# Seven products in place of eight for four rows of a mixer, and weight sums made by transfers

## The chip, the cores and the metric

The kernel runs on one core of a Trainium2 chip. The metric is the device time of one launch in microseconds (us). The core has five engines that run side by side and wait for one another by semaphores: PE (TensorE, matmuls), DVE (VectorE), ACT (ScalarE), POOL (GpSimd, here mostly an issuer of transfers) and SP (SyncE, here only an issuer of transfers).

## The reference, cut to what matters

Two layers of a streaming encoder. Each layer is a half-step feed-forward net, a mixer, and a second half-step feed-forward net. The mixer computes, with `h = RMSNorm(x)` and `z = h @ w_in` split into columns for the convolution, the attention and the gates:

```python
g = jax.nn.sigmoid(g + b_gate)
g_conv, g_attn = jnp.split(g, 2, axis=-1)
y_conv, conv_new = _short_conv(cb, cc, cv, conv_prev, w_conv)
...
y_attn, k_new, v_new = attn_fn(q, k, v)
y_attn = y_attn.reshape(b, t, ATTN_W)
m = g_conv * (y_conv @ w_conv_out) + g_attn * (y_attn @ w_attn_out)
return m @ w_o, conv_new, k_new, v_new
```

There are 640 tokens (512 of a new stream and 8 x 16 of running ones), 1024 model columns, and 512 columns each of convolution and attention. All is float32.

## The kernel before

**Tiling.** Activations lie transposed: 128 columns of the model on the partitions, the 640 tokens (`T`) along the row, in two halves of 320 (`HT`). The eight row tiles of the model are numbered m = 0 to 7. Each float32 operand is split into a high part that the matmul reads exactly (`hi`, made by a cast on ACT) and the remainder (`lo`, made by a subtraction on DVE), and a product is the sum of three matmuls: hi x hi, hi x lo, lo x hi.

**Weights.** All weights come through one stream `wst` of slabs, each 128 x 1024 float32 (512 KB, eight 128 x 128 tiles), which SP loads into three `raw` buffers in the order in which they are used. `load` issues the transfer; `source` says which pieces make up the i-th slab that PE uses; `prep` issues the casts to `whi`; `flush` the subtractions to `wlo`; `slab` hands out the next one and prepares two further ones; `ahead` asks for the sources of the one after that.

**Products by seven.** Where two row tiles of output are computed together, the kernel replaces the eight half-width products of a 2 x 2 block scheme by seven (Winograd's form of Strassen's method). Such a unit has two raw slabs ("mix" in the list of slabs) and four slabs for PE: the first raw slab as it is, two sums of weights, one sum and one plain half, and the last plain half. It also needs sums and differences of the activations (`N6`, `T5`, `T7`, `T4`), made once in a layer. In `source`, a unit of a mixer makes four 512-wide sums on DVE. Many units of the feed-forward nets (`lean`) have one of their sums made by two transfers on POOL, the second of which adds into the tile that the first has filled (`lend`).

**The stage in question.** `outputs` runs after attention, once in each layer. Its scheduled engines are PE, DVE and ACT: they work in the order in which the code issues, and POOL and SP follow by their waits. It has two kinds of step:

- `gate_pair(m)`: two row tiles of gates by seven products, `block` being one of them (12 matmuls); copies c1, u2 and c5 on ACT, additions and a multiplication by `rr` (the inverse norm) on DVE, then two sigmoids on ACT.
- `out(m)`: a plain product of a row tile, `product(py, y)`, with 4 x 3 x 2 = 24 matmuls; then DVE multiplies it by its gate. For m below 8 it is the convolution and goes into `mm[m]`; for m from 8 it is the attention and is added to `mm[m - 8]`. `py` has two PSUM buffers (`acc`).

The order is: gate pair 2; plain products 0 to 3; then for m = 4, 6, ..., 14 a gate pair m and the plain products m and m + 1. `take` splits the operands of the plain products into hi and lo, inside gate pair 2 for the convolution and inside gate pair 8 for the attention; `give` does it with `mm` for the product with `w_o` that follows (`po`). `mm[0]` to `mm[3]` reuse the convolution's own tiles `ycs`, and `mm[4]` to `mm[7]` are two spare tiles.

Of the kernel before, what the change touches and what calls it, by code (L numbers as in the profile page):

```python
# [16 lines left out]
P = 128  # L17
# [40 lines left out]
ROWS = (1, 2)  # L58

MARGIN = 2, 4  # L60
LEAN = {"a0": (1, 6), "b0": (1, 5), "a1": (0, 5), "b1": (1, 5)}

XT4, XN6, XT7, X21, X22, X11, XT5 = range(7)
# [50 lines left out]
def mixer_order():  # L114

    mix = lambda *rows: ("mix", rows)
    out = [("v", None)] + [mix(("q", p), ("k", p)) for p in range(AW // P)]
    for c in range(0, CT, 2):  # L120
        out += [mix(("C", c + i), ("V", c + i)) for i in range(2)] + [mix(("B", c), ("B", c + 1))]
    gates = [mix(("g", m), ("g", m + 1)) for m in range(0, 2 * KT, 2)]
    out += gates[:2] + [("co", m) for m in range(4)]
    for i, g in enumerate(gates[2:]):
        name, m = ("co", 4 + 2 * i) if i < 2 else ("ao", 2 * i - 4)
        out += [g, (name, m), (name, m + 1)]
    return out + [("o", m) for m in range(KT)]


# [6 lines left out]
def stages():  # L136

    out, done = [], []

    def end(kind):  # L140
        done.append((kind, out[:]))
        out.clear()

    def plain(n):
        out.extend([8] * (n // 8) + [n % 8] * (n % 8 > 0))

    def ffn(name):
        held = 0
        for what, a in ffn_order(name):
            if what == "gu":  # L150
                plain(held)
                held = 0
                out.append("gu")
            elif what == "std":
                held += 2 * KT
            elif what == "cut":
                plain(held)
                held = 0
            elif what == "rows":
                plain(held)  # L160
                held = 0
                out.append("gu")
            elif what == "ends":
                held += KT * len(a)
            else:
                held += sum(len(js) for _, js in a)
        plain(held)

    for l in range(L):
        ffn(f"a{l}")  # L170
        end("ffn")
        held = 0
        for what, _ in mixer_order():
            if what == "mix":
# [21 lines left out]
def trunk(ctx: ExitStack, tc: tile.TileContext, xin, wst, small, pbias, samplebias, kcache, vcache, gfin,  # L196
# [54 lines left out]
    for kind, units in stages():  # L251
        n = sum(2 if z in ("gu", "mix") else 1 for z in units)
        if kind == "ffn":
            inner.update(range(at + MARGIN[0], at + n - MARGIN[1]))
        at += n
    raws, ready = [], []
    sums, pool, spool = {}, [None], [None]
    lent, lean, at = {}, set(), 0
    for name, (_, units) in zip([f"{k}{l}" for l in range(L) for k in "amb"], stages()):
        ns = []  # L260
        for z in units:
            if z == "gu":
                ns.append(at)
            at += 2 if z in ("gu", "mix") else 1
        if name in LEAN:
            lean.update(ns[slice(*LEAN[name])])

    def lend(n):

        z = lent[n] = pool[0].tile([P, 2, HT], F32, tag="cap", name=f"lent{n}", bufs=6).rearrange(  # L270
            "p a b -> p (a b)")[:, h1]
        POOL.dma_start(z, wst[n][:, h1])
        POOL.dma_start(z, wst[n + 1][:, h1], accum_op=ALU.add)

    def load(i):
        while len(raws) <= i:
# [16 lines left out]
    def source(i):  # L293

        if i >= len(slabs):
            return None
        if i not in sources:
            kind, n, arg = slabs[i]
            ra = load(n)
            if kind == "plain":  # L300
                sources[i] = [(ra, slice(0, arg))]
            elif arg == 0:
                if n in lean and n not in lent:
                    lend(n)
                sources[i] = [(ra, whole)]
            else:
                rb = load(n + 1)
                if arg == 1 and kind == "gu":
                    if n + 2 in lean:
                        lend(n + 2)  # L310
                    st = sums[n] = pool[0].tile([P, CH], F32, tag="s65", name=f"s65_{n}", bufs=1)
                    add(st[:, h2], rb[:, h1], rb[:, h2])
                    add(st[:, h1], st[:, h2], ra[:, h1])
                    sources[i] = [(st, whole)]
                elif arg == 1:

                    flush()
                    st = sums[n] = spool[0].tile([P, CH // 2], F32, tag="s6", name=f"s6_{n}", bufs=1)
                    add(ra[:, h1], ra[:, h1], rb[:, h1])
                    add(st, ra[:, h1], rb[:, h2])  # L320
                    add(rb[:, h1], rb[:, h1], rb[:, h2])
                    sources[i] = [(st, h1), (rb, h1)]
                elif arg == 2:
                    if kind == "gu" and n not in lean:
                        add(ra[:, h1], ra[:, h1], rb[:, h1])
                    add(ra[:, h2], sums.pop(n)[:, h1], ra[:, h2])
                    sources[i] = [(lent.pop(n), h1), (ra, h2)] if n in lean else [(ra, whole)]
                else:
                    sources[i] = [(rb, h2)]
        return sources[i]  # L330

    pending = []
# [984 lines left out]
    def mixer(l, after):  # L1317
        with tc.tile_pool(name=f"yp{l}", bufs=1, reuse_waits="tile") as yp, \
# [84 lines left out]
            with tc.tile_pool(name=f"gp{l}", bufs=1, reuse_waits="tile") as gp, \  # L1403
                 tc.manual_schedule(engines=ORDERED):
                hold[0] = True
                mo = outputs(l, gp, ops.X, st, cs, ycs, yas, sigmoid, gates)
        ex = after()
        with tc.manual_schedule(engines=ORDERED):
            hold[0] = True
# [56 lines left out]
        def t5(self, kp):  # L1466
            self.parts(*(z[:, HT:] for z in self.h[2 * kp]), self.a[kp][:, 1])

    def outputs(l, gp, X, st, cs, ycs, yas, sigmoid, gates):
# [4 lines left out]
        mm = ycs + [spare[i // 2][:, i % 2] for i in range(CT)]  # L1474
# [4 lines left out]
        def gate_pair(m, then=None):  # L1479
# [5 lines left out]
            ACT.copy(c1, pa)  # L1485
# [7 lines left out]
            ACT.copy(u2, pa)  # L1493
            block(pc, s1, 1, XT5, every, True, True)
            ACT.copy(c5, pc)
            s2 = slab(True)[0]
# [5 lines left out]
            if then:  # L1502
                then()
            block(pc, s2, 1, X22, every, False, True)
            add(u[:, t2], pc, u2)
            s3 = slab(True)[0]
            DVE.tensor_tensor(out=u, in0=u, in1=rr, op=ALU.mult)
# [5 lines left out]
            DVE.tensor_tensor(out=g[:, t1], in0=pa, in1=rr[:, t1], op=ALU.mult)  # L1513
            sigmoid(g, m + 1, -1.0)
            flush()

        def parts(pool, tag, name, src):
# [3 lines left out]

        def out(m, y, then=None):

            py = acc(f"py{l}_{m}")
            product(py, y)
            if then:
# [7 lines left out]
            flush()  # L1534

        yc, ya, mo = [], [], []

        def take(y, name, srcs):
            for c, src in enumerate(srcs):
                y.append(parts(gp, f"y{c}", f"{name}{l}_{c}", src))  # L1540

        def give(ms):
            for m in ms:
                mo.append(parts(hp, "h", f"m{l}_{m}", mm[m]))

        gate_pair(2, lambda: take(yc, "yc", ycs))
        for m in range(4):
            out(m, yc)
        for m in range(4, 2 * KT, 2):
            last = m == 2 * KT - 2  # L1550
            gate_pair(m, (lambda: take(ya, "ya", [yas[:, c, :] for c in range(CT)])) if m == KT else
                      (lambda: give(range(1))) if last else None)
            y = yc if m < KT else ya
            out(m, y, (lambda: give(range(1, 4))) if last else None)
            out(m + 1, y, (lambda: give(range(4, 6))) if last else None)
        give(range(6, KT))
        return mo

# [518 lines left out]
def _stream(i):  # L2077
# [9 lines left out]
    for l in range(L):  # L2087
# [36 lines left out]
        for what, m in mixer_order():  # L2124
            if what == "v":
                out.append(v.reshape(KT // 2, 2, P, AW).transpose(0, 2, 1, 3).reshape(-1, P, CH))
            elif what == "mix":
                out.append(chunks(held))
                held = []

                out.append(chunks([rows[name][a][o::2] for name, a in m for o in range(2)]))
            else:
                held.append(rows[what][m])
        out.append(chunks(held))
# [71 lines left out]
```

## Time and profile before

| | us |
|---|---|
| three runs | 2488.77, 2489.51, 2489.75 |
| median | 2489.51 |
| the profiled execution | 2488.93 |
| its span, first to last instruction | 2487.1 |
| DVE busy in the span | 2140.1 |
| ACT busy in the span | 1355.4 |

The profile is of one execution. Times inside it count from the first instruction. A row of a timeline has start, length, engine, line, operation and tiles, and in square brackets how long the engine stood idle before it and what ended that. A busy PE isn't PE at its peak, since the ends of matmuls are modelled and they overlap; starts are better than durations there. The mean granted clock of TensorE was 0.999.

### The profile page before, as it was taken

The numbers are of one execution on the slowest core, as the hardware profiler recorded it, in microseconds if no ns is written. First come the engines' busy times: TensorE is split into PE (matmuls) and PEld (weight loads), VectorE is DVE, ScalarE is ACT, GpSimd is POOL, SyncE is SP. The second block draws the span as 40 slices with busy tenths as digits, with TensorE's granted clock in tenths as the row PEclk, the third lists the DMA queues.
The fourth block names the chain that finished last, engine by engine and source line by source line (L and its number), as shares of the span: only waits on it lengthen the run. The fifth ranks groups of instructions, "written<-read, shape, count | busy, mean of one in ns | idle before, by whom it ended". The sixth has DMA issues, their size and how long they took to land.

```text
span 2487.1 us, 43918 instructions
## 1 busy us (share of the span) xinstructions
PE 2473.8 (99%) x17312; PEld 2421.2 (97%) x17312; DVE 2140.1 (86%) x3533; ACT 1355.4 (54%) x2152; POOL 298.4 (12%) x451
## 2 busy tenths in 40 slices
PE   9999999999999999999999999999999999999999
PEld 8999999889999999999999999998999999999998
DVE  7999998888776899998799999988886769999997
ACT  6555556665444655555665555556644455555555
POOL 0111112211000001111001011121110000111111
PEclk9999999999999999999999999999999999999999
DMA  4443545335223333444334443453442232444444
GB/s 155 126 118 101 124 118 121 113 108 174 77 82 114 93 102 105 113 117 117 111 93 109 110 118 101 116 128 106 133 157 86 77 111 87 109 116 105 113 117 117
DMA packets 109934, 279.75 MB, mean 112 GB/s; under 512 B 12480, under 2 KB 52032, under 8 KB 109728
## 3 DMA queue, kind: packets, MB, share of 16 engines
q1 hardware_dynamic: 69552, 220.10, 28.0%
q0 software_dynamic: 39744, 56.60, 12.3%
q8 instruction: 135, 2.21, 0.4%
q14 instruction: 71, 0.58, 0.1%
q10 hardware_dynamic: 432, 0.25, 0.0%
HBM read 231.09 MB, written 7.94 MB: 96 GB/s over the span
## 4 chain that ended last, share of the span: by engine, by line
PE 94%; DVE 3%; ACT 2%; issue 1%; DMA 1%; SPq 0%; DVEq 0%; ACTq 0%; POOLq 0%
PE pab L442 12%; PE paa L442 11%; PE pcb L442 6%; PE daa L1127 6%; PE pca L442 5%; PE dab L1127 5%; PE po L418 5%; PE py L418 5%; PE qa L442 4%; PE pbb L442 3%; PE dca L1127 3%; PE pba L442 3%; PE dcb L1127 2%; PE ma_cv L442 2%; PE ma_qk L442 2%; PE pv L1612 2%
## 5 line engine op out<-in xcount | busy, mean ns | idle before, releaser
L352 DVE TENSOR_TENSOR wlo<-raw,whi 128x1024 fp32r<-128x1024 f32 (+1 forms) x569 | 579.9, 1021 | 155.9 <-ACT whi L347 152.8
L347 ACT CAST whi<-raw 128x1024 fp32r<-128x1024 f32 (+1 forms) x569 | 504.7, 890 | 380.1 <-PE pbb L442 47.2
L347 ACT CAST whi<-s 128x1024 fp32r<-128x1024 f32 (+1 forms) x158 | 150.3, 951 | 296.1 <-issue 111.2
L442 PE MATMUL pab<-xhib,whi 128*128 128x320 f32 x704 | 217.7, 309 | 0.0
L442 PE MATMUL pab<-xhib,wlo 128*128 128x320 f32 x704 | 217.3, 309 | 0.0
L442 PE MATMUL pab<-xlob,whi 128*128 128x320 f32 x704 | 217.3, 309 | 0.0
L442 PE MATMUL paa<-xhia,whi 128*128 128x320 f32 x640 | 197.8, 309 | 0.2 <-DVE ga L287 0.2
L442 PE MATMUL paa<-xhia,wlo 128*128 128x320 f32 x640 | 197.6, 309 | 0.0
L442 PE MATMUL paa<-xloa,whi 128*128 128x320 f32 x640 | 197.5, 309 | 0.0
L352 DVE TENSOR_TENSOR wlo<-s,whi 128x1024 fp32r<-128x1024 f32 (+1 forms) x158 | 173.5, 1098 | 4.6 <-ACT whi L347 4.6
L1149 POOL DMA_DIRECT2D x<-c_a x80 | 70.2, 1030 | 574.1 <-ACT ahia L1031 205.4
L442 PEld LDWEIGHTS pab<-xhib,whi 128*128 128x128 f32 x704 | 132.2, 188 | 0.9 <-issue 0.9
L1149 POOL DMA_DIRECT2D x<-c_b x72 | 63.2, 1013 | 582.0 <-ACT ahib L1031 205.6
L442 PEld LDWEIGHTS pab<-xlob,whi 128*128 128x128 f32 x704 | 132.2, 188 | 0.0
L442 PEld LDWEIGHTS pab<-xhib,wlo 128*128 128x128 f32 x704 | 132.2, 188 | 0.0
L442 PEld LDWEIGHTS paa<-xhia,whi 128*128 128x128 f32 x640 | 120.1, 188 | 1.1 <-DVE ga L287 0.5
L442 PEld LDWEIGHTS paa<-xloa,whi 128*128 128x128 f32 x640 | 120.2, 188 | 0.3 <-DVE xloa L686 0.3
L442 PEld LDWEIGHTS paa<-xhia,wlo 128*128 128x128 f32 x640 | 120.1, 188 | 0.2
L442 PE MATMUL pcb<-xhib,wlo 128*128 128x320 f32 x352 | 108.9, 309 | 0.0
L442 PE MATMUL pcb<-xlob,whi 128*128 128x320 f32 x352 | 108.6, 309 | 0.0
L442 PE MATMUL pcb<-xhib,whi 128*128 128x320 f32 x352 | 108.6, 309 | 0.0
L287 DVE TENSOR_TENSOR raw<-s,raw 128x512 f32<-128x512 f32 x158 | 107.9, 683 | 0.0
(764 smaller groups left out, 8077.7 us busy)
## 6 DMA issues: line engine op xcount, KB each, us to landing
raw<-in_wst SPq DMA_DIRECT2D x375, 512.0 KB, 3.6
x<-c_a POOLq DMA_DIRECT2D x80, 160.0 KB, 4.7
x<-c_b POOLq DMA_DIRECT2D x72, 160.0 KB, 3.6
lent<-in_wst POOLq DMA_DIRECT2D x36, 256.0 KB, 3.9
kc<-in_kcache SPq DMA_DIRECT2D x32, 256.0 KB, 4.9
vc<-in_vcache SPq DMA_DIRECT2D x16, 512.0 KB, 4.9
x<-u_a POOLq DMA_DIRECT2D x40, 160.0 KB, 3.9
x<-u_b POOLq DMA_DIRECT2D x36, 160.0 KB, 3.9
```

Source lines behind the costliest of these rows:

```text
L287: DVE.tensor_tensor(out=out, in0=a, in1=b, op=op)
L347: ACT.copy(hi[:, d], src[:, c])
L352: DVE.tensor_tensor(out=lo, in0=src, in1=hi.bitcast(F32), op=ALU.subtract)
L418: PE.matmul(ps[:, a, :HT], w, x[a] if isinstance(x, tuple) else x[:, a * HT : (a + 1) * HT], start=first and j == 0 and not seeded, stop=l ...
L442: PE.matmul(ps, a, b, start=start and kp == 0 and j == 0, stop=stop and kp == NP - 1 and j == 2, skip_group_check=True)
L1127: PE.matmul(ps[u], w, y, start=start and i == 0 and j == 0, stop=i == 1 and j == 2, skip_group_check=True)
L1149: POOL.dma_start(x[ms[2 * u + r]][:, cols], z[:, u], accum_op=ALU.add)
L1612: PE.matmul(pv[t], xx[:, t * P : (t + 1) * P], w[:, kk * AW : (kk + 1) * AW], start=c == 0 and kk == 0 and j == 0, stop=c == KT // 2 - 1 a ...
```

## The change

**Order.** `mixer_order` puts the convolution's rows 4 to 7 together after gate pairs 4 and 6, as one unit `("rows", ("co", (4, 5, 6, 7)))` that is laid out and listed as a seven-product unit. The order of the stage becomes: gate pair 2; plain products 0 to 3; gate pair 4; gate pair 6; the rows unit; then four times a gate pair (8, 10, 12, 14) and two plain products. The weight bytes of the stream stay the same.

**The rows unit.** `rows` computes four output rows by seven products of 12 matmuls over half the tokens, in place of four plain products. The stages s1, s2 and s5 hold what ACT copies out of PSUM; DVE adds and multiplies by the gates in place, and ACT copies the four results to `mm[4]` to `mm[7]` at the start of gate pair 8.

```diff
+        def rows(name, ms, y):
...
+            def mul(ps, s, half, k, start):
+                for u in range(2):
+                    for i in range(2):
+                        kp = half * NP + 2 * u + i
+                        wh, wl = (z[:, kp * P : (kp + 1) * P] for z in s)
+                        xh, xl = kind(y, i, k)
+                        for j, (w, x_) in enumerate(((wh, xh), (wh, xl), (wl, xh))):
+                            PE.matmul(ps[u], w, x_, start=start and i == 0 and j == 0,
+                                      stop=i == 1 and j == 2, skip_group_check=True)
...
+            w = quiet()
+            mul(a, w, 0, X11, True)
+            ACT.copy(s1, two(A))
+            due()
+            prep(used[0] + 1)
+            flush()
+            mul(b, w, 1, X21, True)
+            add(s1, two(B), s1)
+            w = slab(True)[0]
+            flush()
+            mul(a, w, 0, XN6, False)
+            ACT.copy(s2, two(A))
+            gated(0, [s1[:, u] for u in range(2)], t1)
+            mul(c, w, 1, XT5, True)
+            for u in range(2):
+                ACT.copy(s5[:, u], c[u])
+            w = slab(True)[0]
+            mul(a, w, 0, XT7, False)
+            add(s5, two(A), s5)
+            flush()
+            ahead()
+            gated(1, [s5[:, u] for u in range(2)], t2, -1.0)
+            mul(c, w, 1, X22, False)
+            for u in range(2):
+                add(s2[:, u], c[u], s2[:, u])
+            w = slab(True)[0]
+            gated(0, [s2[:, u] for u in range(2)], t2)
+            mul(a, w, 0, XT4, False)
+            flush()
+            gated(1, a, t1, -1.0)
+            if name == "co":
+                lates.append(lambda: [ACT.copy(mm[m], g) for m, g in zip(ms, gs)])
```

**The mixtures.** The rows unit needs sums and differences of the convolution's own operands. `mixed` makes them in place in `ycp`, for two pairs of tiles, in steps that are placed in the plain products 0 to 3 (ahead of each product's multiplication by its gate) and in gate pair 4:

```diff
+        def mixed(i, y, z):
+
+            z = z.rearrange("p c (a b) -> p (c a) b", a=2)
+            e1, e2, o1, o2 = (z[:, i] for i in range(4))
+            add(e1, e1, e2, ALU.subtract)
+            add(e2, o2, e2, ALU.subtract)
+            for out, a in ((o2, e1), (o1, o2)):
+                DVE.scalar_tensor_tensor(out=out, in0=a, scalar=-1.0, in1=out, op0=ALU.mult, op1=ALU.subtract)
+            yield
+            hi, lo = (gp.tile([P, 3, HT], F32R, tag=f"x{i}{p}", name=f"x{p}{l}_{len(more)}") for p in ("hi", "lo"))
+            ACT.copy(hi, z[:, 1:])
+            more.append((hi, lo))
+            yield
+            low(lo, z[:, 1:], hi)
+            yield
...
+        gate_pair(2, [none, none, lambda: take(yc, "yc", range(CT), ycs)])
+        z = [mixed(i, yc, ycp[i]) for i in range(2)]
+        out(0, yc, going(z[0]))
+        out(1, yc, also(going(z[0]), going(z[1])))
+        out(2, yc, also(going(z[0]), going(z[1])))
+        out(3, yc, going(z[1]))
+        both = also(going(z[0]), going(z[1]))
+        gate_pair(4, [both, none, both])
+        gate_pair(6, [none] * 3)
+        rows("co", (4, 5, 6, 7), yc)
```

As the convolution's tiles are in use for that, `mm[0]` to `mm[3]` are now the spare tiles and `mm[4]` to `mm[7]` the old `ycs`.

**Weight sums by transfers.** From gate pair 4 on, all seven units of each layer's stage are `lean`: the sums called `three` (of the second raw slab's two halves) and `one` (of the two first halves) are made by two transfers each on POOL, and DVE makes two 512-wide sums of a unit instead of four.

```diff
+    def lend_part(n, tag, second=False):
+
+        k, c = {"three": ((n + 1, h1), (n + 1, h2)), "one": ((n, h1), (n + 1, h1))}[tag][second]
+        if not second:
+            lent[n, tag] = apart[0].tile([P, CH // 2], F32, tag=tag, name=f"{tag}{n}", bufs=1)
+        POOL.dma_start(lent[n, tag], wst[k][:, c], **({"accum_op": ALU.add} if second else {}))
+
+    def lend_rest(n):
+        for tag, second in (("one", False), ("three", True), ("one", True)):
+            lend_part(n, tag, second)
...
+                elif arg == 1 and n in lean:
+                    three = lent.pop((n, "three"))
+                    st = sums[n] = spool[0].tile([P, CH // 2], F32, tag="s6", name=f"s6_{n}", bufs=1)
+                    add(st, three, ra[:, h1])
+                    sources[i] = [(st, h1), (three, h1)]
...
+                if arg > 1 and kind == "mix" and n in lean and after_mix[n] in lean:
+                    lend_part(after_mix[n], "three") if arg == 2 else lend_rest(after_mix[n])
```

Each tile has one buffer, so the transfers of a unit wait until the unit before has read it. The first unit's four are issued at the start of `outputs`.

**Sigmoids.** `gate_pair` no longer issues its two sigmoids itself; they go into the list `lates`, which `due` runs at the start of the next plain product, or in the next gate pair or rows unit after its first ACT copy.

```diff
             ACT.copy(c1, pa)
+            due()
             prep(used[0] + 1)
             flush()
+            at[0]()
...
-            sigmoid(u, m)
+            lates.append(lambda: sigmoid(u, m))
...
-            sigmoid(g, m + 1, -1.0)
+            lates.append(lambda: sigmoid(g, m + 1, -1.0))
```

More of the change, by code (lines that the diff above doesn't have):

```diff
@@ L255, in trunk @@
         at += n
+    mixes = [n for kind, n, arg in slabs if kind == "mix" and arg == 0]
+    apart = [None]
+    after_mix = dict(zip(mixes, mixes[1:] + [None]))
     raws, ready = [], []
@@ L302, in source @@
             elif arg == 0:
-                if n in lean and n not in lent:
+                if kind == "gu" and n in lean and n not in lent:
                     lend(n)
@@ L1544, in give, with low @@
                 mo.append(parts(hp, "h", f"m{l}_{m}", mm[m]))
[L1546 to L1549, printed above, removed]
-            last = m == 2 * KT - 2
[L1551 to L1555, printed above, removed]
+        def low(lo, z, hi):
+            DVE.tensor_tensor(out=lo, in0=z, in1=hi.bitcast(F32), op=ALU.subtract)
@@ new lines, in mixed @@
+        def mixed(i, y, z):
[12 more added lines that the diff above has]
+            yield
+            hi, lo = (u[:, t2] for u in y[2 * i])
+            ACT.copy(hi, e1)
+            yield
+            low(lo, e1, hi)
+            yield
@@ new lines, in outputs @@
+        out(3, yc, going(z[1]))
[3 more added lines that the diff above has]
+        rows("co", (4, 5, 6, 7), yc)
+        for m in range(KT, 2 * KT, 2):
+            last = m == 2 * KT - 2
+            gate_pair(m, [none, none, (lambda: take(ya, "ya", range(CT), yas_)) if m == KT else
+                          (lambda: give(range(1))) if last else none])
+            out(m, ya, (lambda: give(range(1, 4))) if last else None)
+            out(m + 1, ya, (lambda: give(range(4, 6))) if last else None)
```

90 lines of the change are left out of this document (72 added, 18 removed).

## The prediction

> **What bounds the kernel now.** I read the page first: which engine is full, and who carries the chain that ended last.
>
> ```profile
> span 2487.1 us, 43918 instructions
> PE 2473.8 (99%) x17312; PEld 2421.2 (97%) x17312; DVE 2140.1 (86%) x3533; ACT 1355.4 (54%) x2152; POOL 298.4 (12%) x451
> ...
> PE 94%; DVE 3%; ACT 2%; issue 1%; DMA 1%; SPq 0%; DVEq 0%; ACTq 0%; POOLq 0%
> ```
>
> TensorE is busy for 99% of the span and carries 94% of the chain, but ends of matmuls are modelled, so "busy" alone proves little. The change touches only the function `outputs`, once in each layer, so I cut that stage out by windows. Columns: stretch, length, then busy time and count of PE, PEld, DVE, ACT, POOL, the granted clock, the DMA share and GB/s.
>
> ```profile
> core 0: us, PE busy (x) PEld busy (x) DVE busy (x) ACT busy (x) POOL busy (x), PEclk, DMA share, GB/s
> 635.60:647.90 12.30, 12.30 (x86) 12.30 (x86) 8.78 (x14) 8.59 (x14) 0.00 (x0) 1.00 0.27 88
> 647.90:661.98 14.08, 14.08 (x98) 14.08 (x98) 11.06 (x16) 6.02 (x8) 0.00 (x0) 1.00 0.22 74
> 661.98:674.28 12.30, 12.30 (x86) 12.30 (x86) 6.99 (x10) 4.85 (x7) 0.00 (x0) 1.00 0.31 91
> ...
> 635.60:778.10 142.50, 142.43 (x973) 142.20 (x972) 102.70 (x147) 66.25 (x97) 0.00 (x0) 1.00 0.26 86
> 1867.40:2009.90 142.50, 142.43 (x973) 142.20 (x972) 102.45 (x147) 66.06 (x97) 0.00 (x0) 1.00 0.26 86
> ```
>
> Layer 0's stage is the fourth row, layer 1's the fifth, and the first three are gate pair 2, the four convolution rows m = 0 to 3 and gate pair 4. VectorE is busy 72% of the stage, POOL not at all. The chain in order of time says how tightly PE runs there (start, length, matmuls in a row).
>
> ```profile
> 635.59 1.76 PE qa L442 x12
> ...
> 647.90 14.08 PE py L418 x96
> ...
> 674.28 7.04 PE py L418 x48
> ...
> 778.09 56.72 PE po L418 x384
> ```
>
> 48 matmuls in 7.04 us are 0.1467 us each; that is the price of a matmul here, not the duration of 309 ns, which overlaps the next one. From 635.59 to 778.09 stand seven gate pairs of 84 matmuls and sixteen plain products of 24: 972 x 0.1467 = 142.6 us against 142.5 measured. So PE never waits in this stage: every matmul taken out is worth its 0.1467 us, no other saving can shorten the stage, and every stall that the change brings is paid in full.
>
> **The change, part by part.** *Rows 4 to 7 by seven.* Four plain products (4 x 24 = 96 matmuls) become seven products over half-width mixtures (7 x 12 = 84). Twelve matmuls fewer in each layer: 12 x 0.1467 = 1.76 us, and 3.52 us for both. The clock is granted in full (1.00), so the price holds.
>
> *Weights of that unit.* Two plain slabs become four slabs, whose casts and low parts are made on ACT and DVE. Priced by these groups (mean ns behind the bar):
>
> ```profile
> L352 DVE TENSOR_TENSOR wlo<-raw,whi 128x512 fp32r<-128x512 f32 x14 | 9.6, 683 | 0.0
> L1513 DVE TENSOR_TENSOR g<-qa,rrm 128x320 f32<-128x320 f32 x7 | 3.4, 489 | 0.1
> L287 DVE TENSOR_TENSOR raw<-raw 128x512 f32<-128x512 f32 x7 | 4.8, 684 | 0.0
> ...
> L1334 ACT ACTIVATE g<-g,sm 128x640 f32<-128x640 f32 x16 | 12.3, 823 | 10.4 <-DVE g L1507 10.4
> L347 ACT CAST whi<-raw 128x512 fp32r<-128x512 f32 x14 | 8.7, 620 | 1.9 <-DVE raw L287 1.0 <-PE qb L442 0.9
> L1485 ACT COPY capsm<-qa 128x320 f32<-128x320 f32 x7 | 3.0, 429 | 23.9 <-PE qa L442 23.9
> ```
>
> *Sums by transfer.* In each of the seven units of a layer from gate pair 4 on, DVE makes two 512-wide sums instead of four: 2 x 0.684 = 1.4 us of DVE less per unit. As PE waits for nothing, it shortens nothing; it pays for the DVE work below.
>
> *Mixtures.* Between the plain products 0 to 3 DVE gets two packets of four 320-wide operations, two 960-wide low parts, and ACT two 960-wide casts. The question is whether that fits before PE needs the accumulator again, since `py` has two buffers: product 2 reuses that of product 0, which is free once DVE has multiplied it by its gate. DVE's timeline there:
>
> ```profile
> 649.50 0.48 DVE L287 TENSOR_TENSOR g<-qc,capsm 128x320 f32<-128x320 f32 x1
> 650.02 0.83 DVE L1507 TENSOR_TENSOR g<-g,rrm 128x640 f32<-128x640 f32 x1
> 650.77 0.48 DVE L1513 TENSOR_TENSOR g<-qa,rrm 128x320 f32<-128x320 f32 x1
> 651.17 1.22 DVE L352 TENSOR_TENSOR wlo<-raw,whi 128x1024 fp32r<-128x1024 f32 x1
> 652.47 0.82 DVE L1530 TENSOR_TENSOR yc<-py,g 128x640 f32<-128x640 f32 x1
> 654.85 1.23 DVE L352 TENSOR_TENSOR wlo<-raw,whi 128x1024 fp32r<-128x1024 f32 x1 [1.55 <-ACT whi L347]
> 655.99 0.82 DVE L1530 TENSOR_TENSOR yc<-py,g 128x640 f32<-128x640 f32 x1
> ...
> 662.02 0.82 DVE L1530 TENSOR_TENSOR yc<-py,g 128x640 f32<-128x640 f32 x1 [1.35 <-PE py L418]
> ...
> 670.87 0.49 DVE L287 TENSOR_TENSOR g<-qa,c 128x320 f32<-128x320 f32 x1 [3.47 <-PE qa L442]
> ```
>
> Starts give the pace: 0.40 us from one 320-wide operation to an independent one (650.77 to 651.17), 0.52 to one that needs its result (649.50 to 650.02), 1.14 after a 1024-wide low part (654.85 to 655.99). Now the multiplication of product 0 ends at 653.29; PE needs the buffer at 647.90 + 2 x 3.52 = 654.94, 1.65 us later. The changed program puts the first packet ahead of it. The packet starts at 651.17 + 1.14 = 652.31, its operations each need the one before: 3 x 0.52 + 0.40 = 1.96, so the multiplication runs from 654.27 to 655.09. PE is held 0.15 us, some 0.2 with the restart. Then 0.73 to the next start, the low part 1.14, the second packet 1.96: multiplication of product 1 from 658.10 to 658.92, where PE wants its buffer at 655.14 + 3.52 = 658.66: 0.3 us more. Packet and low part fit in the idle 1.55 and 1.35 us only in part. After that DVE has made everything by about 667, and its 3.47 us of idleness in gate pair 4 take up the rest. Cost 0.5 us a layer. From below: with operations 0.41 apart, as three mixtures of the feed-forward stage are, both multiplications end in time and the cost is nothing. From above, 0.57 is the widest gap there:
>
> ```profile
> 891.76 0.48 DVE L1086 SCALAR_TENSOR_TENSOR dob<-deb,dob 128x320 f32<-128x320 f32 x1
> 892.17 0.48 DVE L1088 TENSOR_TENSOR dob<-dob,deb 128x320 f32<-128x320 f32 x1
> ...
> 916.60 0.48 DVE L1088 TENSOR_TENSOR dob<-dob,deb 128x320 f32<-128x320 f32 x1
> 917.17 0.83 DVE L1076 TENSOR_TENSOR alob<-dob,ahib 128x640 fp32r<-128x640 f32 x1
> ```
>
> Four times 0.57 makes 0.5 and 0.6 us late; with restarts I take 1.5 a layer as the top. I take 0.5, because the 0.52 is of the same kind, an operation reading the one before it.
>
> *The unit itself and what follows.* Let R be its start on PE. ACT's tightest queue is in gate pair 8 (from R + 12.32): it copies c1 at 14.1, then the four finished rows into `mm`, three casts, and only then u2, which PE needs out of the way at 12.32 + 4 x 1.76 = 19.36. With ACT's paces (640-wide below; a copy of 0.43 and a cast of 0.62 start 0.32 and 0.53 before the next):
>
> ```profile
> 643.99 0.73 ACT L234 CAST yc_0hi<-yc 128x640 fp32r<-128x640 f32 x1
> 644.62 0.73 ACT L234 CAST yc_1hi<-yc 128x640 fp32r<-128x640 f32 x1
> ```
>
> 14.14 + 0.32 + 4 x 0.63 + 3 x 0.53 + 0.43 = 19.0. It fits by 0.36 us, provided that DVE has finished row 7 by 16.3; I add up its queue to 15.9. Cost nothing; without that cover what it is late by. Behind the waiting copies stand the casts of gate pair 8's third slab, then u2 and c5, and PE waits for those.
>
> *Sigmoids and casts moved.* The two sigmoids of a pair are put off to the start of the next plain product or past the next pair's copy of c1. They take 0.82 us each, the multiplication that reads them comes 3.52 us after that start, and between pairs no one reads them for a whole pair: nothing. The 960-wide casts fall into the 14.08 us of the plain products, where ACT is busy for 6.02: nothing, and if they came late the low parts behind them would only delay multiplications whose buffers are needed by no one until the rows unit.
>
> *Transfers.* 28 more on POOL in each layer, 256 KB each, the second of a pair held in POOL's queue until the first has landed. POOL has nothing else to do there, SP's loads lie on another queue, and the stage's DMA share of 0.26 roughly doubles. How long such transfers take:
>
> ```profile
> L272 POOL DMA_DIRECT2D lent<-in_wst x18: 543/566/770, 6.3 to 2090.5; - x18
> L273 POOL DMA_DIRECT2D lent<-in_wst x18: 865/874/927, 12.2 to 2094.8; - x18
> ...
> DMA to landing us min/median/max: 3.0/3.9/7.3
> ...
> DMA to landing us min/median/max: 3.0/5.0/5.4
> ```
>
> The third line is for all 36 of them, the last for the four between 785 and 835. The tightest pair is that of gate pair 8's `three`: the tile is free when DVE has read it, about R + 1.8; two transfers of 3.9 land at R + 9.6; DVE adds it at R + 10.7 (the seventh-term product ends at 8.8, then 0.06, 0.73 and 1.14 of its queue). Slack 1.1 us, cost nothing at the median. At 5.0 each the sum would be 1.1 late and PE, by the ACT queue above, about 0.7 a layer.
>
> The Trainium skill ("DMA: Bandwidth & Descriptors", "Anatomy of one DMA") gives about 2.0 us plus bytes over 436 GB/s for such a transfer, which makes 2.6 us at 256 KB, by estimate. By that the pair would land at R + 7 and the sum stay as it is with wider slack; the fastest of the 36 took 3.0, so the trace is slower, and I keep the trace.
>
> *Sum.* -3.52 + 2 x 0.5 = -2.5 us: span 2487.1 to 2484.6, and the profiled execution, which took 2488.93 with what lies around the span, to 2486.4. The median of the runs shown, 2489.51, is 0.58 above that execution: forecast 2487.0. With no stall 2486.0; with 1.5 a layer from the mixtures and 0.7 from the late pair, -3.5 + 4.4 = +0.9, 2490.4.
>
> **The rivals.** *Everything hidden.* The mixtures run at 0.41 and PE never waits: 2489.5 - 3.5 = 2486.0. For it: ACT's four sigmoids now start earlier, so the 1.55 us wait at 654.85 may vanish. Against it: every operation of a packet waits for the one before.
>
> *Transfers come late (the slower side).* Place: POOL's pairs for gate pair 6, the rows unit and gate pair 8, the only units that follow one another without plain products. Needed: landing times above 5.2 us each; at 5.4 gate pair 8 gets its sum 1.9 late and PE loses 1.5 a layer, so +0.5, 2490.0. At the maximum of 7.3 the three sums come 3.7, 2.2 and 5.7 late; less about 1.2 each that DVE's idle time covers, 8 us a layer, 16 - 2.5 = +13.5, 2503. Slower by over 0.2% begins near 6.2. Against it: the median, and a DMA share of 0.26 in this stage. The Trainium skill ("SBUF — State Buffer", "SBUF: two separate sides") warns that a two-port mode of VectorE can shut POOL out of writing descriptors; the issues beside busy DVE took 0.54 to 0.93 us above, without such a hold.
>
> *ACT is jammed in gate pair 8* by the four copies: 0.36 us of slack are within my reading error; 0.5 to 1 a layer gives 2488 to 2489.
>
> *Nothing is saved,* because PE was waiting anyway: excluded by 142.6 against 142.5. *More than 3.5 us is saved:* nothing else of PE's work goes, and no wait is there to lose.
>
> **How the numbers follow.** Forecast with its stall of 0.5 a layer 0.50, all hidden 0.20, ACT jam 0.13, late transfers 0.13 (half of it beyond 6.2 us), all else 0.04 (half of it faster, the rest mostly slower). A measurement of this kernel can tell about 0.2%, or 5 us, from no change: faster would be below 2484.5, more than the whole saving, slower above 2494.5. So faster 0.02, slower 0.065 + 0.015 = 0.08, same 0.90. Range: from all hidden less the spread of single runs (1 us between lowest and highest), 2485.0, to the upper sum and a little of the late transfers, 2491.0.
>
> **What would show it.** Right: 24 matmuls fewer; the stage 141.2 us long; PE waits of 0.2 to 0.3 us before the third and fourth plain product, for DVE's multiplication into `mm`; none in the rows unit. Wrong: DVE waiting for a transfer in the weight sums (late transfers), PE waiting for ACT's copy of u2 in gate pair 8 (jam), a stage of 140.7 (all hidden), or a matmul price other than 0.1467.

## The result and the profile after

| | median us | lowest to highest, runs | ratio to before, 95% interval |
|---|---|---|---|
| before | 2488.97 | 2488.59 to 2490.04, 18 | |
| after | 2493.72 | 2492.36 to 2495.86, 18 | 1.0019 [1.0012, 1.0027] |

The change costs 4.75 us. That is 0.19%, right at the 0.2% which the prediction called measurable, but the interval leaves out 1; the forecast was 2487.0 and its range ended at 2491.0. The page of the profiled execution after:

```profile
span 2491.2 us, 44033 instructions
PE 2473.8 (99%) x17288; PEld 2418.4 (97%) x17288; DVE 2148.9 (86%) x3573; ACT 1372.3 (55%) x2196; POOL 337.6 (14%) x507
...
PE 88%; DVE 5%; issue 2%; DMA 2%; ACT 2%; POOL 0%; SPq 0%; DVEq 0%; POOLq 0%; ACTq 0%
```

The 24 matmuls are gone (17312 to 17288), yet the span is 4.1 us longer. PE's share of the chain of waits fell from 94% to 88%; DVE, transfers and issues took it over. The stage, cut out by windows as before (from the first matmul of gate pair 2 to the first of `po`), in layer 0 and layer 1:

```profile
core 0: us, PE busy (x) PEld busy (x) DVE busy (x) ACT busy (x) POOL busy (x), PEclk, DMA share, GB/s
...
635.68:780.57 144.89, 142.54 (x963) 140.65 (x961) 107.12 (x167) 74.76 (x119) 17.82 (x25) 1.00 0.46 128
1869.69:2013.91 144.22, 142.19 (x963) 140.63 (x961) 107.25 (x167) 74.89 (x119) 17.87 (x25) 1.00 0.47 128
```

Counted in this way the stage before is 142.66 us in both layers, and less 12 matmuls (1.76) it would be 140.90. So 3.99 us are lost in layer 0 and 3.32 in layer 1, and -3.52 + 7.31 = +3.8 accounts for most of the change; the rest of the span is longer by 0.3 us. DVE got 4.4 us of work more in the stage and still has 37 us to spare: it isn't full, it is late. What PE waited for (the view of waits, whole run; us in total, times, longest):

```profile
PE qa L466 <- DVE wlo L376: 1.7, 2, 0.9
PE qa L466 <- ACT capsm L1531: 1.6, 2, 0.8
...
PE py L442 <- DVE mm L1569: 0.4, 2, 0.2
PE qa L466 <- ACT capsm L1521: 0.3, 1, 0.3
```

None of the four was there before. The third is the stall foreseen between the plain products; the others are all in gate pair 8: two at its third product (its first matmul, and its first matmul with `wlo`) and one ahead of its fifth, which needs u2 copied out of PSUM. The four sum to 4.0 of the 7.31 us. The view counts a wait from the modelled end of the matmul before; by starts each gap is some 0.15 us longer, and about 0.1 us more goes at the restart behind it. In layer 0 another 0.33 us lie in the rows unit, where the prediction expected none. The waits of gate pair 8 go back to two operations of DVE, the sum `s` for the rows unit (688.53) and the one for gate pair 8 (701.86):

```profile
688.53 0.69 DVE L300 TENSOR_TENSOR s<-three,raw 128x512 f32<-128x512 f32 x1 [2.15 <-DMA three<-in_wst]
...
697.64 1.22 DVE L376 TENSOR_TENSOR wlo<-raw,whi 128x1024 fp32r<-128x1024 f32 x1
701.86 0.69 DVE L300 TENSOR_TENSOR s<-three,raw 128x512 f32<-128x512 f32 x1 [3.00 <-DMA three<-in_wst]
```

DVE stands for 2.15 and then 3.00 us before the weight sum, because the adding transfer into `three` has not landed. DVE works in the order of the code, so the gating of the rows and the low parts queue up behind. The chain of waits through the place shows how one delay feeds the next (start, length, what):

```profile
682.02 6.49 DMA three<-in_wst
...
688.53 0.69 DVE s L300
...
690.80 1.29 DVE wlo L376 x2
...
692.39 0.57 POOL three L282
...
696.00 5.83 DMA three<-in_wst
...
701.86 0.69 DVE s L300
...
709.42 0.42 ACT capsm L1531
709.88 2.03 PE qa L466 x12
```

From bottom to top: PE starts its fifth product of gate pair 8 when ACT has copied u2 (709.42); ACT is late because DVE's gating, whose results it copies first, stands behind DVE's sum (701.86); that waits for a transfer of 5.83 us; the first of this pair could only be issued at 692.39, when DVE had read the one buffer of `three`; and DVE read it late because the adding transfer of the pair before had taken 6.49 us.

### The profile page after: what moved, and what is told of

It is laid out like the page before. It is cut to its first block, busy times and chain, and to the rows that moved or that the text cites. A ratio compares the mean times of both kernels' runs of the same rounds, so it can differ in the third digit from the quotient of the medians.

```text
span 2491.2 us, 44033 instructions
## 1 busy us (share of the span) xinstructions
PE 2473.8 (99%) x17288; PEld 2418.4 (97%) x17288; DVE 2148.9 (86%) x3573; ACT 1372.3 (55%) x2196; POOL 337.6 (14%) x507
## 4 chain that ended last, share of the span: by engine, by line
PE 88%; DVE 5%; issue 2%; DMA 2%; ACT 2%; POOL 0%; SPq 0%; DVEq 0%; POOLq 0%; ACTq 0%
PE pab L466 12%; PE paa L466 11%; PE pcb L466 6%; PE daa L1151 6%; PE pca L466 5%; PE dab L1151 5%; PE po L442 5%; PE pbb L466 3%; PE dca L1151 3%; PE pba L466 3%; PE dcb L1151 2%; PE ma_cv L466 2%; PE ma_qk L466 2%; PE py L442 2%; PE pv L1769 2%
## 5 line engine op out<-in xcount | busy, mean ns | idle before, releaser
L371 ACT CAST whi<-raw 128x1024 fp32r<-128x1024 f32 (+1 forms) x559 | 491.9, 884 | 366.4 <-PE pbb L466 46.0
L376 DVE TENSOR_TENSOR wlo<-raw,whi 128x1024 fp32r<-128x1024 f32 (+1 forms) x559 | 565.4, 1014 | 135.5 <-ACT whi L371 132.2
```

What stands on the lines that cost most here:

```text
L371: ACT.copy(hi[:, d], src[:, c])
L376: DVE.tensor_tensor(out=lo, in0=src, in1=hi.bitcast(F32), op=ALU.subtract)
```

## The experiments

All are the kernel after with one thing changed, unless said otherwise. "Lost" is the length of the stage above 140.90 us in layers 0 and 1, from one profiled execution each. The kernel before was run again beside each group of them, at a median of 2488.93 to 2489.03. The kernel after has 18 runs, e5 has 6 and the others have 11. Every run of e1, e2, e3, e6, e10 and e13 to e15 is faster than the fastest of the kernel after; those of e4, e5 and e7 overlap with it, so there the difference of the medians is less sure.

| | median us | ratio to before, 95% | lost, us |
|---|---|---|---|
| after | 2493.72 | 1.0019 [1.0012, 1.0027] | 3.99, 3.32 |
| e1 sums on DVE | 2490.60 | 1.0007 [0.9998, 1.0015] | 2.49, 2.49 |
| e2 transfers alone | 2489.39 | 1.0001 [0.9992, 1.0010] | none, against 142.66 |
| e4 mixtures after | 2491.99 | 1.0013 [1.0004, 1.0021] | 3.36, 2.91 |
| e5 `three` only | 2497.21 | 1.0032 [1.0020, 1.0044] | 4.86, 7.04 |
| e3 second buffer | 2488.97 | 1.0001 [0.9993, 1.0010] | 0.82, 1.51 |
| e6 spaced | 2490.85 | 1.0007 [0.9999, 1.0016] | 2.65, 2.49 |
| e7 no copies | 2492.14 | 1.0014 [1.0005, 1.0023] | 3.75, 2.49 |
| e10 no transfers, mixtures after, no copies | 2490.14 | 1.0006 [0.9997, 1.0014] | 2.15, 2.15 |
| e13 = e3 + e4 | 2487.58 | 0.9996 [0.9987, 1.0005] | 3.98, 0.93 |
| e14 = e3 + e4 + e7 | 2487.40 | 0.9994 [0.9986, 1.0003] | 1.10, 0.00 |
| e15 no adding | 2489.67 | 1.0004 [0.9995, 1.0013] | 1.54, 2.23 |

### Sums back on DVE (e1)

```diff
-FREE = AW // P + 3 * CT // 2 + 2
+FREE = 10 ** 6
...
-        lend_part(after_mix[slabs[used[0]][1]], "three")
-        lend_rest(after_mix[slabs[used[0]][1]])
```

> The change with the mixers' weight sums back on DVE (no transfers on POOL in this stage). Late-transfer theory: with no transfer to wait for, PE loses only the 0.83 us a layer at the plain products, and at most about 1 us a layer because DVE has 1.4 us more per unit: 2487 to 2489.5, no wait of over 0.5 us in gate pair 8. Overload theory (DVE and ACT have too much to do in the rows unit and gate pair 8, copies and mixtures included, whatever the transfers do): 1.4 us more of DVE work per unit makes it worse, 2494 to 2497, with the waits of gate pair 8 still there.

Measured 2490.60: 3.1 us less than the kernel after, though DVE has more to do, so the transfers did cost time. It is also 1.1 us above the range that I gave for the transfers alone being late. From its waits of PE:

```profile
PE qa L466 <- ACT capsm L1529: 1.4, 2, 0.7
...
PE py L442 <- DVE mm L1567: 0.4, 2, 0.2
```

The waits for `wlo` are gone; the copy of u2 still comes 0.7 us late in each layer, without any transfer.

### The transfers without the rest (e2)

The order of before (plain products 4 to 7, no rows unit, no mixtures), with the transferred sums and the deferred sigmoids kept.

```diff
-    out += gates[:2] + [("co", m) for m in range(4)] + gates[2:4] + [("rows", ("co", (4, 5, 6, 7)))]
-    for i in range(4):
-        out += [gates[4 + i], ("ao", 2 * i), ("ao", 2 * i + 1)]
+    out += gates[:2] + [("co", m) for m in range(4)]
+    for i, g in enumerate(gates[2:]):
+        name, m = ("co", 4 + 2 * i) if i < 2 else ("ao", 2 * i - 4)
+        out += [g, (name, m), (name, m + 1)]
...
```

> The kernel before with the transferred weight sums alone: eight plain convolution rows, no mixtures, gate pairs each followed by two plain products, sigmoids put off as in the change. Late-transfer theory: every unit has 7 us of plain products ahead of it, so a sum that lands late is still in time: 2488.5 to 2490, no wait of PE in the stage, though the second transfer of a pair takes 5 us or more when another is in flight. Rival (the added traffic itself costs, by delaying SP's weight loads): 2490.5 or more, with waits for raw.

As the late-transfer theory expected: 2489.39, and no gap of PE in the stage, whose window reads

```profile
635.36:778.01 142.65, 142.58 (x975) 142.35 (x973) 95.24 (x141) 66.86 (x103) 14.89 (x21) 1.00 0.44 122
```

Here too POOL waited up to 7.6 us for a transfer to land. But two plain products (7.04 us) stand between any two of these units, and none of DVE's waits there names a transfer. The same kind of transfers, 24 in a layer, cost nothing that can be told here; in the kernel after, where units follow each other, they do.

### The mixtures behind each multiplication (e4)

```diff
-        out(0, yc, going(z[0]))
+        out(0, yc, after=going(z[0]))
```

and so for products 1 to 3; `out` runs `after` behind its multiplication and `flush`.

> The change with the steps of the mixtures put behind each plain product's multiplication by its gate instead of ahead of it. The stall at the third and fourth plain product (0.83 us a layer in the profile) goes, the rest stays: 2493.7 - 1.7 = 2492.0. If the mixtures' work then pushes the next units instead, no gain: 2493 to 2494.

Measured 2491.99, as expected: 1.7 us less in the median. The gaps before the third and fourth plain product vanish, those of gate pair 8 stay (0.74, 1.03 and 0.92 us).

### Only `three` by transfers (e5)

```diff
-        for tag, second in (("one", False), ("three", True), ("one", True)):
-            lend_part(n, tag, second)
+        lend_part(n, "three", True)
```

with the sum `one` on DVE.

> The change with only the sum `three` by transfers; the sum `one` is made on DVE, so 14 transfers a layer in place of 28 and never two of POOL's in flight at once. If the long landing comes from two POOL transfers in flight together, the second transfer of a pair lands after 3.7 to 4.5 us instead of 5.5 to 7.3, DVE waits for `three` less than 1 us in the rows unit, PE loses 0 to 1 us a layer in gate pair 8: 2488 to 2490. If an adding transfer takes 5.5 us beside SP's loads by itself, the wait stays at 2 to 3 us: 2492.5 to 2494.

Both theories missed: 2497.21, the slowest of all. With only one transfer of POOL in flight the adding transfer for gate pair 8 took 7.6 us, where the kernel after has 5.8, and DVE stood accordingly:

```profile
702.05 0.69 DVE L299 TENSOR_TENSOR s<-three,raw 128x512 f32<-128x512 f32 x1 [3.80 <-DMA three<-in_wst]
```

The view of transfers over 694 to 702 us says what ran beside it (queue: packets, MB, share of the 16 engines; then the issues, KB each, us to landing):

```profile
q1 hardware_dynamic: 288, 1.05, 36.6%
q0 software_dynamic: 144, 0.26, 23.0%
...
raw<-in_wst SPq DMA_DIRECT2D x2, 512.0 KB, 5.2
three<-in_wst POOLq DMA_DIRECT2D x1, 256.0 KB, 7.6
```

SP had issued one load of 512 KB at 694.04, 0.43 us ahead of the adding transfer (694.47), and issued a second at 695.38: 1.05 MB of raw slabs against 0.26 MB. So a queue of POOL's own transfers isn't needed to make one late. From gate pair 6 on, the twelve adding transfers of this run, each without another of POOL's beside it, sort by the start of SP's first load: 3.7 to 4.3 us where it starts 1.3 us or more behind (six), 5.2 to 5.5 where it starts 0.0 to 0.7 behind (three), and 7.3 to 7.6 where it starts 0.2 to 0.4 ahead (three: gate pair 8 in layer 0, the rows unit and gate pair 8 in layer 1). The Trainium skill ("DMA: Bandwidth & Descriptors", "Issuing engines are not separate DMA queues") says that transfers of all issuing engines run on the same 16 engines and interleave; the trace agrees (these 7.3 to 7.6 us against 3.7 to 4.3), and my "SP's loads lie on another queue" was no cover.

### A second buffer for `three` (e3)

The tile alternates with the slot of `s6`; the sum that stood there is made in place in the raw tile.

```diff
...
+            pl, tg = (spool[0], "s6") if tag == "three" and turn[0] % 2 else (apart[0], tag)
+            lent[n, tag] = pl.tile([P, CH // 2], F32, tag=tg, name=f"{tag}{n}", bufs=1)
...
-                    st = sums[n] = spool[0].tile([P, CH // 2], F32, tag="s6", name=f"s6_{n}", bufs=1)
-                    add(st, three, ra[:, h1])
+                    flush()
+                    st = sums[n] = ra[:, h1]
+                    add(st, three, st)
```

> The kernel after with a second buffer for the tile `three`: it alternates with the slot of `s6`, and the sum that stood there is made in place in the raw tile. So the transfers of a unit's `three` no longer wait for the multiplication of the unit before it, but are written as before. Theory `landing` (the time goes where DVE waits for the adding transfer, which lands late beside SP's loads): DVE no longer waits for `three` in the rows unit and gate pair 8, the gaps before the third and fourth products of gate pair 8 shrink to what remains of ACT's queue, 2489.5 to 2491. Rival `queue` (POOL's transfers are late because they stand one behind the other in one queue, whatever the buffers): DVE still waits for `three` or for `one` in that place, 2493 or more.

`Landing` holds, and the time lies 0.5 us below the range that it gave: 2488.97, which is 4.75 us less than the kernel after. The transfers are no quicker (up to 7.5 us), only earlier (gate pair 8's pair is issued from 678.17 on, not from 692.39), and DVE's two sums start without a wait:

```profile
685.79 0.69 DVE L302 TENSOR_TENSOR raw<-three,raw 128x512 f32<-128x512 f32 x1
...
697.91 0.69 DVE L302 TENSOR_TENSOR raw<-three,raw 128x512 f32<-128x512 f32 x1
```

The `flush` ahead of the sum changes nothing at these two places: here and in the kernel after, DVE's last operation before the sum is the same low part. In layer 0 the three gaps of gate pair 8 vanish, that of u2 too, with the four copies still in place. In layer 1 one of 0.46 us is left. (The expectations here and for e7 number gate pair 8's products otherwise; the gaps that they mean stand at its third and fifth product.)

### Transfers only where plain products stand between (e6)

```diff
-FREE = AW // P + 3 * CT // 2 + 2
+FREE = AW // P + 3 * CT // 2 + 2 + 4
...
```

(and none issued at the start of `outputs`), so that gate pairs 10, 12 and 14 alone have them.

> The kernel after, with sums by transfers only for the units of gate pairs 10, 12 and 14, each of which follows plain products; the units before them have their sums on DVE as before the change. Theory `place` (transfers cost time only where units follow each other without plain products between them): no more than with all sums on DVE, 2490.0 to 2491.1. Rival (transfers cost time wherever they run): between that and the kernel after, 2491.5 to 2493.

2490.85, as `place` expected: no more than with none (e1, 2490.60), within the spread of the runs.

### Without the four ACT copies (e7)

```diff
...
+                    z = mm[ms[2 * r + u]][:, t]
                     if scale is None:
-                        DVE.tensor_tensor(out=g, in0=src[u], in1=g, op=ALU.mult)
+                        DVE.tensor_tensor(out=z, in0=src[u], in1=g, op=ALU.mult)
...
-            if name == "co":
-                lates.append(lambda: [ACT.copy(mm[m], g) for m, g in zip(ms, gs)])
```

> The kernel after, with the four finished rows written by DVE's last gating multiplications straight into the tiles mm, and so without the four ACT copies that follow the rows unit. Theory `ACT queue` (in gate pair 8 the copies hold up the copy u2 and the weight casts): the gap before the third product of gate pair 8 (0.93 us) goes, those before the first and second, which stand behind a late transfer, stay: some 2 us in two layers less, 2491.5 to 2492. Rival `transfers alone`: the copies only stand in idle time and everything behind them waits for the late `three`; the time stays at 2493.2 to 2494.

2492.14, a little above what `ACT queue` gave. The gap ahead of the fifth product (u2) shrinks from 0.93 to 0.16 us. In layer 0 the two at the third product stay (0.60 and 1.03 us), and one of 0.56 us came up in the rows unit; in layer 1 the 1.03 us stays.

### No transfers, mixtures after, no copies (e10)

> The rows unit alone with its two rivals for time taken away: all weight sums of the stage on DVE (no transfers there), the mixtures' steps behind each plain product's multiplication, and the four finished rows written straight by DVE (no ACT copies). If the three causes are the whole loss, they add up: the kernel with DVE sums took 2490.6; the stalls at the plain products (0.83 us a layer) and the stall behind ACT's queue (0.95 a layer) go, so 2490.6 - 1.7 - 1.9 = 2487.0, below the kernel before by about 2 us. If something else of the change costs time (a rival), 2489 or more, with gaps at other places.

This one has the edits of e1, e4 and e7 together. Missed by 3.1 us: 2490.14. The losses don't add up without the transfers: in each layer there are gaps of 0.56 us in gate pair 4, where the rest of the mixtures is made, 0.26 in gate pair 6 and 0.65 in gate pair 8, and the view of waits names ACT's copy of u2 for the first and the last. I put them down to DVE's two sums more in each unit and the ACT casts behind those; no run tests that alone.

### Both losses taken away (e13, e14)

> The kernel with a second buffer for `three` and the mixtures' steps behind each plain product's multiplication: both losses taken away. With the second buffer alone it took 2488.97, with gaps of 0.6 us a layer left before the second and third plain... products; those go here, so if the losses add up, 2488.97 - 1.2 = 2487.8, the matmuls' saving shown at last. If moving the mixtures back makes the rows unit or gate pair 8 late instead, 2488.8 or more.

> The same without the four ACT copies of the finished rows (DVE writes them straight into mm). If the copies only ever stood in ACT's idle time, the same as with them, within 0.5 us; if they still hold up a cast in gate pair 8, another 0.5 to 1 us less, 2486.8 to 2487.3, faster than the kernel before by about 2 us.

With the transfers kept, they do add up: 2487.58 and 2487.40, where 2487.8 was expected. The copies make no difference that can be told. (The profiled execution of e13 is the slowest of its runs, 2490.65: in gate pair 8 of layer 0 the transfers into `one` came so late that PE lost 2.5 us.) In layer 1 of e14 the whole saving stands, 142.66 - 1.76 = 140.90; layer 0 has one gap left:

```profile
635.38:777.38 142.00, 141.10 (x963) 140.61 (x961) 107.66 (x167) 72.56 (x115) 18.63 (x26) 1.00 0.48 134
1866.47:2007.37 140.90, 140.83 (x962) 140.60 (x961) 107.66 (x167) 72.66 (x115) 17.80 (x25) 1.00 0.46 131
```

It is now the other tile, `one`, still with one buffer, for which ACT waits there:

```profile
704.67 0.62 ACT L374 CAST whi<-one 128x512 fp32r<-128x512 f32 x1 [3.60 <-DMA one<-in_wst]
```

Both medians lie 1.4 to 1.6 us below the kernel before, but both intervals hold 1: they beat the kernel after, and that they beat the kernel before isn't shown.

### The second transfer plain instead of adding (e15)

This kernel leaves out one half of each of these weight sums, so it tells of the time alone.

```diff
-        POOL.dma_start(lent[n, tag], wst[k][:, c], **({"accum_op": ALU.add} if second else {}))
+        POOL.dma_start(lent[n, tag], wst[k][:, c], **{})
```

> The kernel after, with the second transfer of each pair in this stage written plainly over the first instead of added to it; so the weight sums of those units lack one half. Bytes, issues, waits and order are the same. Theory `adding` (a transfer that adds takes longer of itself): the second transfers land in 3 to 3.5 us, DVE's waits before the rows unit and gate pair 8 go, 2489 to 2490. Theory `sharing` (they take longer since SP's loads of 512 KB run beside them): they still land after 5 to 7 us, and the time stays at 2493 to 2494.

The time is what `adding` expected (2489.67), the landings are not. The same two transfers in its chain of waits, and then DVE's sum ahead of gate pair 8 in its timeline:

```profile
681.81 5.33 DMA three<-in_wst
...
694.37 4.72 DMA three<-in_wst
```

```profile
699.11 0.69 DVE L300 TENSOR_TENSOR s<-three,raw 128x512 f32<-128x512 f32 x1 [0.89 <-DMA three<-in_wst]
```

In layer 0 the four second transfers for gate pair 6, the rows unit and gate pairs 8 and 10 land after 4.8, 5.3, 4.7 and 5.3 us, where adding took 5.5, 6.5, 5.8 and 7.3; the firsts of the same pairs took 3.0 to 3.4. In layer 1 the same four take 3.7, 5.1, 5.4 and 4.3, where adding took 5.5, 5.9, 5.8 and 7.0. So between these two executions adding costs 0.4 to 2.7 us, and the place, with loads of SP and another transfer of POOL in flight, up to some 2 us more than a first. Neither theory alone is right. About 1 us less in each pair won back 4 of the 4.75 us: DVE's waits ahead of the rows unit and gate pair 8 fell from 2.15 and 3.00 us to 1.06 and 0.89, the second by more than its own transfer gained, since the first handed on less. That SP's loads are enough to make a transfer late e5 shows; how much POOL's other transfer adds was not taken apart.

## Why the prediction was wrong, step by step

**PE is the bound, and a matmul is worth 0.1467 us: right.** 24 are gone, and where no stall is left (e14, layer 1) the stage is shorter by exactly 12 of them.

**Mixtures: right in mechanism, a little short in size.** The multiplication of product 0 was put at 654.27; it started at 654.53, in a stage that starts 0.25 later. Its hold on PE is the row below, and the gaps of 0.38 and 0.23 us, with 0.11 for the restart behind each, make 0.83 a layer where I had 0.5; moving the mixtures back (e4) won 1.7 us in all, which is twice that.

```profile
655.40 0.56 PE L442 MATMUL py<-yc_0hi,whi 128*128 128x320 f32 x2 [0.21 <-DVE mm L1569]
```

**Transfers: the step that failed** is "Slack 1.1 us, cost nothing at the median". This term of the sum was put at nothing; the gaps of gate pair 8, with their restarts, took 2.8 us in layer 0 and 2.5 in layer 1. R, the start of the rows unit on PE, is 687.48, and three numbers went into the slack:

- The tile was to be free at R + 1.8; POOL could issue at 692.39, R + 4.9, 3.1 us later. 2.15 of that is DVE's own wait for the rows unit's `three`: I reckoned gate pair 8's pair as if the one before it were in time. Without that wait DVE has read the tile at about R + 2.5 (e3), so the rest is mostly my reckoning of DVE's queue.
- Two transfers were to take 7.8 us, they took 9.4 (692.39 to 701.83). The 3.9 was the median of first and adding transfers together, over other stages. The kind alone would not have told: the 18 adding ones of the kernel before have a median of 4.0. The slowest of them, 7.3, is one that had two loads of SP beside it nearly all along, for 7.0 and 5.0 us; gate pair 8's had two, for 2.4 and 5.5 of its 5.8 us.
- DVE was to need the sum at R + 10.7 and stood ready at R + 11.4, 0.7 later, which helped.

Together: -1.1 + 3.1 + 1.6 - 0.7 = 2.9 us late, against the 3.00 that the row shows. The gaps of gate pair 8 in layer 0 (0.51, 1.03 and 0.93 us) sum to 2.5, so lateness passes to PE nearly in full, as the rival said.

**The rival "transfers come late" is what happened,** at its place and by its mechanism; it had a chance of 0.13. It put the need at landing times of 5.2 us each, but by the prediction's own sum the slack is gone at 4.45 (1.8 + 2 x 4.45 = 10.7). The pair took 3.3 and 5.8, and with the 0.3 us between them that alone would be 0.5 us late; what the rival lacked at such times was the lateness handed on by the single buffer. As the second buffer alone brings the kernel back to the time of before (e3), and transfers behind plain products cost nothing that can be told (e2, e6), this is shown. The trace of before held the warning in its spread (3.0 to 7.3), and I trusted the middle of it.

**ACT "fits by 0.36 us": on the edge.** The jam came here behind the late sum:

```profile
702.66 0.62 ACT L371 CAST whi<-s 128x512 fp32r<-128x512 f32 x1 [6.22 <-DVE s L300]
...
704.59 1.35 ACT L1683 COPY yc<-g 128x640 f32<-128x640 f32 x2 [0.46 <-DVE g L1647]
706.60 1.36 ACT L1683 COPY yc<-g 128x640 f32<-128x640 f32 x2 [0.66 <-DVE g L1649]
707.86 0.61 ACT L371 CAST whi<-one 128x512 fp32r<-128x512 f32 x1
...
709.42 0.41 ACT L1531 COPY capsm<-qa 128x320 f32<-128x320 f32 x1
```

ACT stood idle for 6.22 us and then had two casts, the copies and three more casts ahead of u2, where PE waited 0.78 us. With the sum in time it fits with all copies in layer 0 (e3) and not quite in layer 1 (0.46 us); with DVE's own sums it doesn't (e1). So that rival is a real but smaller part, and mostly follows from DVE's lateness.

**Sigmoids deferred: nothing,** as said (e2 keeps them so). POOL's issues in the stage took 0.56 to 0.91 us, as in the kernel before (0.54 to 0.93), so the hold that the prediction weighed isn't seen there; one issue ahead of each stage took 1.2 us, and why is open. The estimate of 2.6 us for a transfer (the Trainium skill, "DMA: Bandwidth & Descriptors", "Anatomy of one DMA") was not reached by any `three` or `one` here; the fastest took 2.9 (e3).

## What to carry to other kernels

Price a transfer by its kind and its place, the adding one that starts beside the loads of the same unit, and not by a median over the run. What to look at is when the loads start: here 1.5 us made the difference between 4 and 7.5 us (e5). Where units follow one another through a tile with one buffer, add up the lateness from unit to unit: 1 us more in each pair made DVE's sums 1.1 and then 2.1 us later (e15 against after). In these runs the added transfers were free behind work that their reader doesn't need, two plain products, and nearly free with a second buffer that lets them start a unit earlier.

## What the runs showed of the hardware

Transfers of 256 KB into `three` took 3.0 to 3.8 us as the first of a pair and 3.8 to 7.3 as the adding second (after); plain seconds took 3.1 to 5.4 (e15). Without another transfer of POOL in flight an adding one took 3.7 to 4.3 us where SP's load of 512 KB started 1.3 us or more behind it, and 7.3 to 7.6 where it started 0.2 to 0.4 us ahead (e5). On POOL the issue of an adding transfer into `three` takes 0.85 to 0.90 us, of a plain one 0.54 to 0.58 (after).

Over their runs the kernels whose path runs through such transfers spread by 2.7 to 4.8 us (e4 2491.22 to 2493.89, e13 2485.82 to 2490.65), those with sums on DVE by 1.0 and 1.2 (e1, e10) and the kernel before by 1.4. That landing times vary between executions would explain it, but with one trace of each kernel it isn't shown.
